# Expert value stage: earlier loads, gates laid out by 16 tokens, and gating four blocks at a time

## Chip, cores and metric

One core of a Trainium2 chip runs the whole kernel in one launch. The metric is the device time in microseconds, the median of repeated runs. A profiled execution of the same program gives the trace.

## The reference, cut to what matters

A decoder layer on 512 tokens of 1024 channels. First comes token mixing (differential attention and an mLSTM beside each other), then channel mixing by an expert retrieval, which is where the change lies:

```python
q = (ht @ w_q).reshape(T, PEER_HEADS, 2, PEER_DKEY // 2)
s = jnp.einsum('thpd,pnd->thpn', q, sub_keys).astype(jnp.float32)
sv, si = lax.top_k(s, PEER_TOPK)
...
eidx = i1 * N_KEYS + i2
g = jax.nn.softmax(cv, axis=-1)
...
act = jax.nn.gelu(jnp.einsum('cd,chkd->chk', hc, uc), approximate=False)   # uc = u_tab[ec]
...
return jnp.einsum('chk,chkd->cd', (gc * act).astype(hc.dtype), vc)         # vc = v_tab[ec]
```

Each token picks 8 x 16 of 16,384 experts. An expert is one row of u (layer 1) and one row of v (the value).

## The kernel before

**Dense and sparse tokens.** For 384 of the tokens (TD) the kernel computes all experts: 128 blocks of 128 experts, each block a product h2 x u, a gelu, a multiplication by the token's gate (zero for experts not chosen) and a product with v. For the other 128 tokens it gathers the chosen rows of u and v with indirect DMAs from POOL, one expert slot at a time, into a ring of four buffers (`gat`); VectorE forms the dot products (`gat<-gat,rows`) and later the sums of values (`accg`). `some(sp, n)` hands out these steps between the dense ones.

**Gates.** In the routing stage, before the value stage, `route` builds for each group of 16 tokens the gates of all experts with one-hot matmuls, four tokens to a PSUM tile. ScalarE evicts each tile to `gstage`, and a DMA writes the group to HBM (`gd`). There are 24 groups of four evictions.

**Layer 1.** The activations of blocks 0 to 71 are computed during routing and stored in HBM (`actd`). Those of blocks 72 to 127 are computed in the value stage.

**The value stage** runs rounds of four blocks, in the order q = 18 to 31 and then 0 to 17. `u_round` makes the activation tile `at` of a round (two buffers): for q of 18 and up by matmuls and a gelu on ScalarE, which is the first half of the stage; for q below 18 by two loads from `actd`, the second half. `v_round` multiplies one block of `at` at a time by its gates, splits the product into a high and a low half of 16 bits (`split`: ScalarE the high half, VectorE the low), loads and splits the 512 KB row block of v (`load_w`, three buffers `raw` shared with u, eight buffers for the split rows), and runs 18 matmuls into six PSUM accumulators (`out_part`). The gates of two rounds come in one load of 1.57 MB (`gblk`, two buffers left of the tag `big`). A gate of one block is every eighth element of that tile. The last round's blocks are kept for `last_part`, which closes the accumulators one by one and normalises the tokens.

All these loads leave from SP in one order. A scheduler sets the order of each engine's instructions when the kernel is built; TensorE's own order is that of the code. Each engine waits in order: what stands behind a waiting instruction waits too.

Of the kernel before, what the change touches and what calls it, by code (L numbers as in the profile page):

```python
# [8 lines left out]
F32 = mybir.dt.float32  # L9
# [62 lines left out]
FILL_H = 8400  # L72


class Ordered:
    """TensorE instructions, issued in the order in which they are written."""
# [26 lines left out]
def body(tc, x, c, w_ada, b_ada, wz, wif, b_if, conv_w, conv_b, lam, subg, mlg,  # L103
# [6 lines left out]
    with pool(name="cst", bufs=1) as cst, pool(name="wts", bufs=1) as wts, \  # L110
            pool(name="keep", bufs=1) as keep, pool(name="bg", bufs=1) as bg, \
            pool(name="wk", bufs=1) as wk, pool(name="dr", bufs=1, space=DRAM) as dr, \
            pool(name="ps", bufs=1, space=PSUM) as psp:

# [3 lines left out]
        def t4(name, shape=(128, 1024), dt=F32):  # L118
            return wk.tile(list(shape), dt, name=name, tag="t4", bufs=4)

        def t2(name, shape=(128, T), dt=F32):
            return wk.tile(list(shape), dt, name=name, tag="t2", bufs=6)
# [16 lines left out]
        # ---- constants  # L139
# [148 lines left out]
        # ---- adaLN modulation columns  # L288
# [44 lines left out]
        with pool(name="fr", bufs=1) as fr:  # L333
# [3 lines left out]
            # ---- LN1, its transposed, modulated, split copy, and the first projection  # L337
# [36 lines left out]
            # ---- small inputs  # L374
# [35 lines left out]
            # ---- projections of h1, as work between the steps of the branches  # L410
# [25 lines left out]
            # ---- differential attention, in steps of one head and one query block  # L436
# [84 lines left out]
            # ---- mLSTM  # L521
# [184 lines left out]
            # ---- merge  # L706
# [23 lines left out]
            # ---- order of the two branches  # L730
# [101 lines left out]
        # ---- PEER: routing and dense gates, beside the first expert activations  # L832
# [50 lines left out]
        with pool(name="rt", bufs=1) as rt:  # L883
# [50 lines left out]
            def route(t):  # L934
# [81 lines left out]
                for g in range(9):  # L1016
# [17 lines left out]
                    if pend is not None:  # L1034
                        pg, o1, ah, B = pend
                        half = stg[0][:, (pg % 2) * 2048:(pg % 2 + 1) * 2048]
                        st = half.rearrange("p (b t e) -> p b t e", b=16, t=16)
                        for q4 in range(4):
                            ps = ps_tr()
                            for k in range(4):  # L1040
# [3 lines left out]
                            A.activation(st[:, :, 4 * q4:4 * q4 + 4, :],  # L1044
                                         ps.rearrange("p t (b e) -> p b t e", b=16), AF.Copy,
# [8 lines left out]
            # ---- output projection, first residual and its two norms  # L1054
# [122 lines left out]
        # ---- PEER: expert outputs, beside the gathered experts of the first tokens  # L1177
# [4 lines left out]
        with pool(name="vp", bufs=1) as vp:  # L1182
            gat = big([128, 4, 1024], F32, "gat")
            accg = vp.tile([128, 1024], F32, name="accg")
            RV = 1.0 / (S_WT * S_V)
            order = list(range(N1 // 4, 32)) + list(range(N1 // 4))
            AT, GB = {}, {}
# [46 lines left out]
            def u_round(q_, rate=SP_U - SP_V):  # L1234
                at = vp.tile([128, 4, TD], F32, name="at", tag="at", bufs=2)
                AT[q_] = at
                if q_ < N1 // 4:
                    for k in range(2):
                        nc.sync.dma_start(at[:, 2 * k:2 * k + 2].rearrange("p a b -> p (a b)"),
                                          actd[2 * q_ + k])  # L1240
                else:
                    for i in range(4):
                        for _ in u_gen(4 * q_ + i, at[:, i]):
                            pass
# [122 lines left out]
```

## Time and profile before

| | |
|---|---|
| median of 3 runs | 1868.15 us (1867.54 to 1870.41) |
| span of the profiled execution | 1869.3 us |
| TensorE matmuls busy in it | 1718.7 us (92%) |
| VectorE busy | 1471.2 us (79%) |
| ScalarE busy | 822.8 us (44%) |
| GpSimd busy | 445.9 us (24%) |
| DMA, mean over the span | 259 GB/s |

The profiled execution is 1.15 us longer than the median of the runs. Shares over the span are means over stages with different limits; the stage of the change is cut out in the rows below.

### The profile page before, as it was taken

To read this page: it belongs to the slowest core of one execution; us is meant where nothing else is said; L and a number is where in the kernel's file an instruction comes from. 1 tells how busy PE (TensorE), PEld (TensorE's weight loads), DVE (VectorE), ACT (ScalarE), POOL (GpSimd) and SP (SyncE) were. 2 spreads that over 40 slices of the span, in tenths; PEclk is the share of its full clock that TensorE was granted. 3 is DMA by queue.
4 is the path that set the end of the run, shared out by engine and by line. 5 is a ranking of instruction groups with operands and counts; after the bars stand their busy time and mean duration, and the time that the engine had idled before them with its cause. 6 is when DMAs were issued, how large, how long until landed. Compare 5 with 4: busy or idle time off the path is not lost.

```text
span 1869.3 us, 26856 instructions
## 1 busy us (share of the span) xinstructions
PE 1718.7 (92%) x9937; PEld 920.4 (49%) x9937; DVE 1471.2 (79%) x2894; ACT 822.8 (44%) x1375; POOL 445.9 (24%) x296
## 2 busy tenths in 40 slices
PE   5999999989999899999989989999998998878895
PEld 2444455454444666666657544544554543333342
DVE  7778786786667798789899576977987777677689
ACT  4556766564343424547557432433332322222332
POOL 0000000010001000111101144544555634334443
PEclk9999999989999899999999999999999999989998
DMA  8555653447784457977959999899998888877874
GB/s 331 175 187 182 235 193 112 142 148 273 279 292 169 161 186 233 318 252 243 305 194 306 347 312 346 321 318 339 340 340 301 303 313 293 307 276 275 287 274 166
DMA packets 185477, 484.92 MB, mean 259 GB/s; under 512 B 15233, under 2 KB 64641, under 8 KB 185345
## 3 DMA queue, kind: packets, MB, share of 16 engines
q1 hardware_dynamic: 87280, 286.05, 44.5%
q0 software_dynamic: 36864, 134.23, 20.0%
q10 hardware_dynamic: 61200, 62.92, 9.8%
q8 instruction: 77, 1.26, 0.3%
q14 instruction: 56, 0.45, 0.1%
HBM read 418.14 MB, written 65.01 MB: 258 GB/s over the span
## 4 chain that ended last, share of the span: by engine, by line
PE 32%; DVE 25%; DMA 18%; issue 13%; POOL 7%; ACT 3%; ACTq 0%; DVEq 0%; POOLq 0%; SPq 0%
PE mm L97 21%; PE s L97 8%; DMA at<-actd 7%; DVE w L163 7%; POOL gat L859 7%; DVE accg L1227 4%; DMA gat<-in_v_dram,ev 4%; DMA gd<-gstage 2%; DVE at L1262 2%; PE tr L97 1%; DVE gat L867 1%; DMA raw<-in_v_dram 1%; PE tr L100 1%; DMA pre<-in_u_dram 1%; DMA gat<-in_urows_dram,eu 1%
## 5 line engine op out<-in xcount | busy, mean ns | idle before, releaser
L97 PEld LDWEIGHTS <-w 128*128 128x128 f16 x7176 | 694.1, 99 | 724.8 <-issue 120.4
L97 PE MATMUL mm<-h2T,w 128*128 128x384 f16 (+2 forms) x3288 | 564.0, 329 | 34.5 <-ACT at L851 22.5
L162 ACT ACTIVATE w<-raw 128x1024 f16<-128x1024 f32 x308 | 322.8, 1054 | 455.1 <-DMA raw<-in_v_dram 359.9
L163 DVE SCALAR_TENSOR_TENSOR w<-raw,w 128x1024 f16<-128x1024 f32 x308 | 375.2, 1220 | 100.2 <-ACT w L162 99.4
L97 PE MATMUL s<-w,w 128*128 128x512 f16 x1152 | 281.8, 389 | 48.5 <-DVE w L163 47.5
L859 POOL DMA_INDIRECT gat<-in_v_dram,ev x128 | 238.5, 1863 | 276.6 <-DVE accg L1227 265.8
L859 POOL DMA_INDIRECT gat<-in_urows_dram,eu x128 | 174.1, 1360 | 478.0 <-DVE gat L867 380.0
L97 PE MATMUL mm<-h1T,w 128*128 128x512 f16 x960 | 220.5, 381 | 1.8 <-DVE cva L618 1.8
L97 PE MATMUL tr<-w,w 128*128 128x512 f16 x768 | 186.2, 379 | 0.0
L1262 DVE TENSOR_TENSOR at<-at,gblk 128x384 f32<-128x384 f32 x128 | 108.6, 852 | 96.1 <-DMA at<-actd 90.0
L1227 DVE SCALAR_TENSOR_TENSOR accg<-gat,wg,accg 128x1024 f32<-128x1024 f32 x127 | 162.9, 1283 | 7.9 <-DMA gat<-in_v_dram,ev 7.8
L162 ACT ACTIVATE w<-at 128x384 f16<-128x384 f32 x128 | 65.7, 514 | 129.7 <-DVE at L1262 123.2
L867 DVE SCALAR_TENSOR_TENSOR gat<-gat,rows 128x1024 f32<-128x1024 f32 x89 | 108.1, 1219 | 12.5 <-DMA gat<-in_urows_dram,eu 12.4
L97 PE MATMUL mm<-w,h1T 128*128 128x512 f16 x456 | 107.7, 382 | 3.3 <-ACT h1T L162 1.8
L97 PE MATMUL o<-w,w 128*128 128x512 f16 x384 | 105.5, 386 | 0.0
L97 PEld LDWEIGHTS <-h1T 128*128 128x128 f16 x672 | 58.2, 98 | 66.0 <-issue 2.8
L159 POOL TENSOR_TENSOR ss<-ss,mhalf 128x4 f32<-128x4 f32 x8 | 8.1, 1017 | 314.4 <-DVE ss L504 283.4
L163 DVE SCALAR_TENSOR_TENSOR pre<-pre 128x1024 f16<-128x1024 f32 x44 | 53.8, 1223 | 34.8 <-ACT pre L162 33.7
L1044 ACT ACTIVATE gstage<-tr 128x512 f32<-128x512 f32 x96 | 56.6, 597 | 50.7 <-PE tr L97 39.6
L306 DVE SCALAR_TENSOR_TENSOR wad<-wad,silc 128x1024 f32<-128x1024 f32 x48 | 58.2, 1220 | 19.9 <-DMA wad<-in_w_ada_dram 19.9
L97 PEld LDWEIGHTS <-onehot 128*128 128x128 f16 x768 | 64.1, 148 | 19.1 <-issue 9.1
L97 PE MATMUL tr<-onehot 128*128 128x128 f16 x768 | 64.6, 227 | 9.0 <-ACT gstage L1044 7.6
(458 smaller groups left out, 1717.6 us busy)
## 6 DMA issues: line engine op xcount, KB each, us to landing
raw<-in_v_dram SPq DMA_DIRECT2D x128, 512.0 KB
raw<-in_u_dram SPq DMA_DIRECT2D x92, 512.0 KB
raw<-in_wz_dram SPq DMA_DIRECT2D x64, 512.0 KB
w<-us SPq DMA_DIRECT2D x52, 512.0 KB
wad<-in_w_ada_dram SPq DMA_DIRECT2D x48, 512.0 KB
gd<-gstage ACTq DMA_DIRECT2D x24, 1024.0 KB
us<-pre ACTq DMA_DIRECT2D x44, 512.0 KB
pre<-in_u_dram SPq DMA_DIRECT2D x36, 512.0 KB
```

Source lines behind the costliest of these rows:

```text
L97: self._link(self.tc.nc.tensor.matmul(*a, **k))
L100: self._link(self.tc.nc.tensor.transpose(*a, **k))
L159: G.tensor_tensor(o, i, mhalf[:, :i.shape[1]], op=ALU.pow)
L162: A.activation(hi, src, AF.Copy, scale=scale)
L163: V.scalar_tensor_tensor(lo, src, scale, hi, op0=ALU.mult, op1=ALU.subtract)
L306: V.scalar_tensor_tensor(w, w, 0.5, silc, op0=ALU.mult, op1=ALU.mult, accum_out=raw_[:, j:j + 1])
L859: P.before(G.indirect_dma_start(out=g_, out_offset=None, in_=table, in_offset=bass.IndirectOffsetOnAxis(ap=e[:, k:k + 1], axis=0)))
L867: V.scalar_tensor_tensor(g_, g_, 1.0, ring["h2r"], op0=ALU.mult, op1=ALU.mult, accum_out=wg[:, k:k + 1])
L1044: A.activation(st[:, :, 4 * q4:4 * q4 + 4, :], ps.rearrange("p t (b e) -> p b t e", b=16), AF.Copy, scale=1.0 / S_G)
L1227: V.scalar_tensor_tensor(accg, g_, wg[:, k:k + 1], accg, op0=ALU.mult, op1=ALU.add)
L1262: V.tensor_tensor(at[:, i], at[:, i], gt_[:, :, 4 * (q_ % 2) + i], op=ALU.mult)
```

## The change

- The scratch tiles of the first part (tags t4 and t2) get a pool of their own, which is closed before the value stage. The stage uses the room for a third buffer of `at` (AT_B = 3) and five buffers `vraw` for the rows of v (V_B = 5), apart from the three `raw` that remain for u.
- `gstage` and `gd` hold the gates by expert and then token: the 16 tokens of a group lie next to each other. The eviction therefore writes runs of four tokens and reads PSUM across four token tiles, one element from each in turn.
- The gates of two rounds are loaded in four parts, and the stored activations in two, from `ahead`, which is called between the value blocks two or three rounds before their use.
- `gate` multiplies all four blocks of a round at once (128 x 1536 instead of four times 128 x 384) and splits them at once into `w`, which has two buffers of a whole round instead of eight of one block. It is called for the next round after the second value block.

```diff
+AT_B = 3
+V_B = 5
...
+        front = ExitStack()
+        wt = front.enter_context(pool(name="wt", bufs=1))
...
-            return wk.tile(list(shape), dt, name=name, tag="t4", bufs=4)
+            return wt.tile(list(shape), dt, name=name, tag="t4", bufs=4)
...
-                        st = half.rearrange("p (b t e) -> p b t e", b=16, t=16)
+                        st = half.rearrange("p (i t) -> p i t", t=16)
...
-                            A.activation(st[:, :, 4 * q4:4 * q4 + 4, :],
-                                         ps.rearrange("p t (b e) -> p b t e", b=16), AF.Copy,
+                            A.activation(st[:, :, 4 * q4:4 * q4 + 4],
+                                         ps.rearrange("p t i -> p i t"), AF.Copy,
...
+        front.close()
...
-            def u_round(q_, rate=SP_U - SP_V):
-                at = vp.tile([128, 4, TD], F32, name="at", tag="at", bufs=2)
-                AT[q_] = at
-                if q_ < N1 // 4:
-                    for k in range(2):
-                        nc.sync.dma_start(at[:, 2 * k:2 * k + 2].rearrange("p a b -> p (a b)"),
-                                          actd[2 * q_ + k])
-                else:
-                    for i in range(4):
-                        for _ in u_gen(4 * q_ + i, at[:, i]):
-                            pass
-                        if q_ == order[0]:
-                            G.tensor_copy(gat[0:1, i, 0:1], at[0:1, i, 0:1])
-                        some(sp, rate)
+            def held(n):
+                return n < len(order) and order[n] < N1 // 4
+
+            def new_at(n):
+                AT[n] = vp.tile([128, 4, TD], F32, name="at", tag="at", bufs=AT_B)
+                return AT[n]
+
+            def act_load(n, k):
+                at = AT[n] if n in AT else new_at(n)
+                nc.sync.dma_start(at[:, 2 * k:2 * k + 2].rearrange("p a b -> p (a b)"),
+                                  actd[2 * order[n] + k])
+
+            def gate_load(n, k):
+                blk = order[n] // 2
+                if blk not in GB:
+                    GB[blk] = big([128, NG, 8, 16], F32, "gblk")
+                gs = slice(k * NG // 4, (k + 1) * NG // 4)
+                nc.sync.dma_start(GB[blk][:, gs].rearrange("p g e t -> p g (e t)"),
+                                  gd[gs, blk].rearrange("g p f -> p g f"))
+
+            def ahead(n, i):
+                if held(n + 2) and i % 2 == 0:
+                    act_load(n + 2, i // 2)
+                if n % 2 == 1 and i > 1 and n + 3 < len(order):
+                    gate_load(n + 3, i - 2)
+                if n % 2 == 0 and i % 2 == 0 and n + 2 < len(order):
+                    gate_load(n + 2, 2 + i // 2)
+
+            def u_round(n, rate=SP_U - SP_V):
+                at = new_at(n)
+                for i in range(4):
+                    for _ in u_gen(4 * order[n] + i, at[:, i]):
+                        pass
+                    if n == 0:
+                        G.tensor_copy(gat[0:1, i, 0:1], at[0:1, i, 0:1])
+                    some(sp, rate)
+
+            def gate(n):
+                q_, at = order[n], AT.pop(n)
+                av = at.rearrange("p a (g t) -> p a g t", t=16)
+                e = slice(4 * (q_ % 2), 4 * (q_ % 2) + 4)
+                V.tensor_tensor(av, av, GB[q_ // 2][:, :, e].rearrange("p g e t -> p e g t"),
+                                op=ALU.mult)
+                w = vp.tile([128, 2, 4, TD], F16, name="w", tag="w", bufs=2)
+                split(w[:, 0], w[:, 1], at, S_WT)
+                WT[n] = w
 
             ACC = [[ps_s(), ps_s()], [ps_s(), ps_o()],
                    [ps_tr().rearrange("p a b -> p (a b)") for _ in range(2)]]
-
-            def v_round(q_, first, keep_ops=None):
-                blk = q_ // 2
-                if blk not in GB:
-                    gt_ = big([128, TD, 8], F32, "gblk")
-                    nc.sync.dma_start(gt_.rearrange("p (g t) e -> p g (t e)", g=TD // 16),
-                                      gd[:, blk].rearrange("g p f -> p g f"))
-                    GB.clear()
-                    GB[blk] = gt_
-                gt_, at = GB[blk], AT[q_]
+            BANKS = [(t, b) for t in range(3) for b in range(2)]
+
+            def load_v(i2):
+                raw = vp.tile([128, 1024], F32, name="vraw", tag="vraw", bufs=V_B)
+                nc.sync.dma_start(raw, v[i2])
+                w = wts.tile([128, 2, 1024], F16, name="w2", tag="w2", bufs=8)
+                split(w[:, 0], w[:, 1], raw, S_V)
+                return w[:, 0], w[:, 1]
+
+            def out_part(op, tiles, start, stop):
+                w, i, vv = op
+                for t, b in tiles:
+                    ts = slice(t * 128, (t + 1) * 128)
+                    s = slice(b * 512, (b + 1) * 512)
+                    mm3_one(ACC[t][b], (w[:, 0, i, ts], w[:, 1, i, ts], vv[0][:, s], vv[1][:, s]),
+                            start, stop)
+
+            def v_round(n, keep_ops=None):
+                w = WT.pop(n)
                 for i in range(4):
-                    V.tensor_tensor(at[:, i], at[:, i], gt_[:, :, 4 * (q_ % 2) + i], op=ALU.mult)
-                    w = vp.tile([128, 2, TD], F16, name="w", tag="w", bufs=W_B)
-                    split(w[:, 0], w[:, 1], at[:, i], S_WT)
-                    op = (w, load_w(v[4 * q_ + i], S_V))
+                    ahead(n, i)
+                    op = (w, i, load_v(4 * order[n] + i))
                     if keep_ops is not None:
                         keep_ops.append(op)
                         continue
-                    out_part(op, BANKS, first and i == 0, False)
+                    out_part(op, BANKS, n == 0 and i == 0, False)
                     some(sp, SP_V)
+                    if i == 1 and n + 1 < len(order):
+                        gate(n + 1)
 
...
-                    o = t4("fo")
+                    o = vp.tile([128, 1024], F32, name="fo", tag="vraw", bufs=V_B)
...
-            u_round(order[0], SP_0)
-            for n, q_ in enumerate(order):
-                if n + 1 < len(order):
-                    u_round(order[n + 1])
+            for k in range(6):
+                gate_load(k // 4 * 2, k % 4)
+            u_round(0, SP_0)
+            gate(0)
+            for n in range(len(order)):
+                if n + 1 < len(order) and not held(n + 1):
+                    u_round(n + 1)
                 if n == 2:
                     P.before(nc.sync.dma_start(lg, ln2g.to_broadcast([128, 1024])))
                     P.before(nc.sync.dma_start(lb, ln2b.to_broadcast([128, 1024])))
-                v_round(q_, n == 0, ops if n == len(order) - 1 else None)
+                v_round(n, ops if n == len(order) - 1 else None)
```

SP's order in the second half of the stage, two rounds before the change. `raw<-in_v_dram` is a row block of v, `gblk<-gd` the gates, `at<-actd` the stored activations:

```order
240 L1256 DMA gblk<-gd 128x24x128
241 L167 DMA raw<-in_v_dram 128x1024 x2
242 L1239 DMA at<-actd 128x768 x2
243 L167 DMA raw<-in_v_dram 128x1024 x4
244 L1239 DMA at<-actd 128x768 x2
245 L167 DMA raw<-in_v_dram 128x1024 x2
```

The same place of the changed kernel, two rounds:

```order
256 L1251 DMA at<-actd 128x768 x2
257 L1295 DMA vraw<-in_v_dram 128x1024 x2
258 L1259 DMA gblk<-gd 128x6x128
259 L1295 DMA vraw<-in_v_dram 128x1024
260 L1259 DMA gblk<-gd 128x6x128 x2
261 L1295 DMA vraw<-in_v_dram 128x1024
262 L1259 DMA gblk<-gd 128x6x128
263 L1251 DMA at<-actd 128x768 x2
264 L1295 DMA vraw<-in_v_dram 128x1024 x4
```

The gate load of two rounds is now spread in quarters between the value rows, and no longer one block a few rows ahead of the activations.

VectorE's order in the second half before the change, most of a round. `at<-at,gblk` is the gating of one block, `w<-at,w` its low half, `w<-raw,w` that of the value rows (printed with the number of its buffer), `accg<-gat,wg,accg` the sum of a gathered row:

```order
2157 L1262 TENSOR_TENSOR at<-at,gblk 128x384
2158 L163 SCALAR_TENSOR_TENSOR w<-at,w 128x384
2159 L163 SCALAR_TENSOR_TENSOR w_15910<-raw,w_15910 128x1024
2160 L1227 SCALAR_TENSOR_TENSOR accg<-gat,wg,accg 128x1024
2161 L163 SCALAR_TENSOR_TENSOR w<-at,w 128x384
2162 L163 SCALAR_TENSOR_TENSOR w_15939<-raw,w_15939 128x1024
2163 L1227 SCALAR_TENSOR_TENSOR accg<-gat,wg,accg 128x1024
2164 L163 SCALAR_TENSOR_TENSOR w<-at,w 128x384
2165 L163 SCALAR_TENSOR_TENSOR w_15968<-raw,w_15968 128x1024
2166 L1227 SCALAR_TENSOR_TENSOR accg<-gat,wg,accg 128x1024
2167 L1262 TENSOR_TENSOR at<-at,gblk 128x384
```

The last split of a round (row 2164) frees its `at`; the next round's first gating (row 2167) follows two instructions later. After the change, one whole round:

```order
1982 L1283 TENSOR_TENSOR at<-at,gblk 128x1536
1983 L169 SCALAR_TENSOR_TENSOR w_15548<-vraw,w_15548 128x1024
1984 L1235 SCALAR_TENSOR_TENSOR accg<-gat,wg,accg 128x1024
1985 L169 SCALAR_TENSOR_TENSOR w_15579<-vraw,w_15579 128x1024
1986 L1235 SCALAR_TENSOR_TENSOR accg<-gat,wg,accg 128x1024
1987 L169 SCALAR_TENSOR_TENSOR w<-at,w 128x1536
1988 L169 SCALAR_TENSOR_TENSOR w_15604<-vraw,w_15604 128x1024
1989 L1235 SCALAR_TENSOR_TENSOR accg<-gat,wg,accg 128x1024
1990 L169 SCALAR_TENSOR_TENSOR w_15631<-vraw,w_15631 128x1024
1991 L1235 SCALAR_TENSOR_TENSOR accg<-gat,wg,accg 128x1024
1992 L1283 TENSOR_TENSOR at<-at,gblk 128x1536
```

A round has one gating and one split, with four instructions between each. The split of row 1987 belongs to the tile that was gated two gatings earlier; it frees the buffer into which the load for the gating of row 1992 goes.

## Rows read from the trace of the kernel before

**Rows 1.** The page's first line.

```profile
span 1869.3 us, 26856 instructions
```

**Rows 2.** Windows: stretch, its length, each engine's busy time (count), TensorE's clock, DMA.

```profile
core 0: us, PE busy (x) PEld busy (x) DVE busy (x) ACT busy (x) POOL busy (x), PEclk, DMA share, GB/s
1040.00:1466.00 426.00, 403.54 (x2152) 212.74 (x2150) 338.27 (x436) 151.37 (x215) 203.10 (x141) 0.98 0.93 328
1466.00:1838.00 372.00, 323.51 (x1445) 143.95 (x1444) 277.55 (x309) 112.39 (x155) 161.32 (x80) 0.95 0.81 289
...
1200.00:1420.00 220.00, 213.98 (x1141) 112.11 (x1140) 188.18 (x237) 80.65 (x113) 113.50 (x77) 0.99 0.94 337
```

**Rows 3.** Waits of TensorE, 1030 to 1870 us: total, times, longest.

```profile
PE s L97 <- DVE w L163: 47.5, 18, 7.2
PE mm L97 <- ACT at L851: 22.5, 6, 5.7
```

**Rows 4.** Waits of VectorE, 1030 to 1870 us.

```profile
DVE at L1262 <- DMA at<-actd: 90.0, 17, 9.4
...
DVE accg L1227 <- DMA gat<-in_v_dram,ev: 7.8, 9, 4.2
```

**Rows 5.** Timeline of SP's issues: start, length, line, transfer.

```profile
1547.04 0.80 SPq L1239 DMA_DIRECT2D at<-actd  x2
...
1660.66 0.68 SPq L1256 DMA_DIRECT2D gblk<-gd  x1
...
1666.67 0.80 SPq L1239 DMA_DIRECT2D at<-actd  x2
1667.81 19.81 SPq L167 DMA_DIRECT2D raw<-in_v_dram  x4
1688.95 0.80 SPq L1239 DMA_DIRECT2D at<-actd  x2
...
1788.27 0.81 SPq L1239 DMA_DIRECT2D at<-actd  x2
```

**Rows 6.** Timeline of VectorE, two rounds; in brackets the idle time before.

```profile
1676.92 0.85 DVE L1262 TENSOR_TENSOR at<-at,gblk 128x384 f32<-128x384 f32 x1 [7.95 <-DMA at<-actd]
...
1688.38 0.55 DVE L163 SCALAR_TENSOR_TENSOR w<-at,w 128x384 f16<-128x384 f32 x1
...
1694.10 0.86 DVE L1262 TENSOR_TENSOR at<-at,gblk 128x384 f32<-128x384 f32 x1 [2.84 <-DMA at<-actd]
```

**Rows 7.** Timeline of TensorE in the same rounds.

```profile
1680.19 3.57 PE L97 MATMUL s<-w,w 128*128 128x512 f16 x8 [6.14 <-DVE w L163]
...
1686.03 2.11 PE L97 MATMUL s<-w,w 128*128 128x512 f16 x9
...
1689.92 2.11 PE L97 MATMUL s<-w,w 128*128 128x512 f16 x9
```

**Rows 8.** Groups by line and form, VectorE, 1466 to 1838 us: busy us, mean ns.

```profile
L1227 DVE SCALAR_TENSOR_TENSOR accg<-gat,wg,accg 128x1024 f32<-128x1024 f32 x81 | 103.9, 1282 | 4.2 <-DMA gat<-in_v_dram,ev 4.2
L163 DVE SCALAR_TENSOR_TENSOR w<-raw,w 128x1024 f16<-128x1024 f32 x76 | 92.8, 1221 | 0.2 <-ACT w L162 0.2
L1262 DVE TENSOR_TENSOR at<-at,gblk 128x384 f32<-128x384 f32 x76 | 64.5, 853 | 90.0 <-DMA at<-actd 90.0
L163 DVE SCALAR_TENSOR_TENSOR w<-at,w 128x384 f16<-128x384 f32 x76 | 42.1, 555 | 0.0
```

**Rows 9.** Groups of VectorE, 600 to 1870 us: other two-operand sums.

```profile
L1194 DVE TENSOR_TENSOR fo<-fo,ax 128x512 f32<-128x512 f32 x6 | 3.9, 685 | 0.0
...
L954 DVE TENSOR_TENSOR cd<-sv 128x128 f32<-128x128 f32 x4 | 1.1, 274 | 0.0
```

**Rows 10.** Groups of ScalarE, 600 to 1870 us.

```profile
L162 ACT ACTIVATE w<-at 128x384 f16<-128x384 f32 x128 | 65.7, 514 | 129.7 <-DVE at L1262 123.2 <-DVE accg L1227 5.7 <-DVE gat L867 0.8
L1044 ACT ACTIVATE gstage<-tr 128x512 f32<-128x512 f32 x96 | 56.6, 597 | 50.7 <-PE tr L97 39.6 <-DMA gd<-gstage 9.0 <-issue 1.6
```

**Rows 11.** Windows: a stretch of gate groups in the routing stage.

```profile
981.92:1002.00 20.08, 20.08 (x185) 14.96 (x184) 20.05 (x22) 13.28 (x21) 2.86 (x2) 1.00 0.87 276
```

**Rows 12.** Timeline of TensorE: one round of layer-1 matmuls.

```profile
1125.94 15.76 PE L97 MATMUL mm<-h2T,w 128*128 128x384 f16 x96
```

More of the change, by code (lines that the diff above doesn't have):

```diff
@@ L1 @@
+from contextlib import ExitStack
 import numpy as np
@@ L118, in t4 @@
         def t4(name, shape=(128, 1024), dt=F32):
-            return wk.tile(list(shape), dt, name=name, tag="t4", bufs=4)
+            return wt.tile(list(shape), dt, name=name, tag="t4", bufs=4)
         def t2(name, shape=(128, T), dt=F32):
-            return wk.tile(list(shape), dt, name=name, tag="t2", bufs=6)
+            return wt.tile(list(shape), dt, name=name, tag="t2", bufs=6)
         def small(name, n, bufs=4, dt=F32):
@@ L1185, in body @@
             RV = 1.0 / (S_WT * S_V)
+            NG = TD // 16
             order = list(range(N1 // 4, 32)) + list(range(N1 // 4))
-            AT, GB = {}, {}
+            AT, WT, GB = {}, {}, {}
             def finish(t, o, halves):
@@ L1279, in last_part @@
                         some(sp, 1000)
-                    o = t4("fo")
+                    o = vp.tile([128, 1024], F32, name="fo", tag="vraw", bufs=V_B)
                     finish(t + 1, o, lambda b, s: V.scalar_tensor_tensor(
                         o[:, s], ACC[t][b], RV, g2r[:, s], op0=ALU.mult, op1=ALU.mult))
-            BANKS = [(t, b) for t in range(3) for b in range(2)]
-            def out_part(op, tiles, start, stop):
-                w, vv = op
-                for t, b in tiles:
-                    ts = slice(t * 128, (t + 1) * 128)
-                    s = slice(b * 512, (b + 1) * 512)
-                    mm3_one(ACC[t][b], (w[:, 0, ts], w[:, 1, ts], vv[0][:, s], vv[1][:, s]),
-                            start, stop)
-            ops = []
-            u_round(order[0], SP_0)
-            for n, q_ in enumerate(order):
-                if n + 1 < len(order):
-                    u_round(order[n + 1])
+            ops = []
+            for k in range(6):
[5 more added lines that the diff above has]
+                    u_round(n + 1)
                 if n == 2:
```

## The prediction

> **What bounds the kernel now.** I first cut the end of the run, the expert value stage, out of the windows view, because every edit but one lies in it. It runs from about 1040 us to the last gather at about 1838 us; the profiled span ends at 1869.3 us [rows 1]. It has two halves [rows 2]. Up to 1466 us each round computes four layer-1 blocks and then four value blocks: TensorE is busy 403.54 of 426 us and DMA moves 328 GB/s at a share of 0.93. After that the layer-1 activations come back from HBM instead: 372 us, TensorE busy 323.51, DMA only 289 GB/s at 0.81. Neither is full in this second half, and that is the thing to explain.
>
> The waits views say who is late. TensorE waits 47.5 us for VectorE's low half of w (all in the second half) and 22.5 us for ScalarE's eviction (all in the first) [rows 3]. VectorE waits 90.0 us for the stored activations, 17 times, and only 7.8 us for gathered rows [rows 4].
>
> One pair of rounds shows why. The activation tile has two buffers, so the next load can only leave when the last tile of the round is split. SP sends it at 1666.67, behind a 1.57 MB gate load sent at 1660.66 in the same queue [rows 5]; VectorE stands 7.95 us until 1676.92, works through the round, splits the last tile at 1688.38 [rows 6]; the next load leaves at 1688.95 [rows 5] and VectorE starts at 1694.10 [rows 6]. So a round is a load, then VectorE's work, one after the other: L + W, with L = 10.25 and 5.15 us (with and without a gate load in front), and W = 1688.95 - 1676.92 = 12.0 us. (10.25 + 5.15) / 2 + 12.0 = 19.7 us, close to the (1788.27 - 1547.04) / 12 = 20.1 us that a round takes from load to load [rows 5]. While VectorE stands, the value rows behind it keep their three buffers, and SP spreads the next four value loads over 19.81 us [rows 5]: one late load dries up the queue. TensorE then sits 6.14 us, and its next 8 matmuls take 3.57 us [rows 7].
>
> The limits, from rows. A value block is 18 matmuls in 1689.92 - 1686.03 = 3.89 us [rows 7], 0.216 us each; a layer-1 matmul takes 15.76 / 96 = 0.164 us [rows 12]. First half: 2152 matmuls [rows 2], of them 1287 layer-1 and the rest value, are 398 us. Second half: 1445, of them 59 layer-1, are 309 us. DMA: 426 x 328 = 139.7 MB and 372 x 289 = 107.5 MB. Where the old loop kept the queue fed, from 1200 to 1420 us, it carried 337 GB/s at 0.94 [rows 2]. At that rate the halves need 415 and 319 us: DMA is the tighter limit in both, TensorE close behind.
>
> **The change, part by part.**
>
> *Three activation tiles, five value row buffers apart from the three that stay for u, quarter gate loads.* Bytes stay the same, and so do the 512 B pieces of the gate load. The order shows what the third tile buys: the load still leaves only after a round's split, but between that split and the gating that needs the load VectorE now has two value splits and two gather sums, 2 x (1.22 + 1.28) = 5.0 us [rows 8], and the gating itself stands two rounds ahead of its split. A round by this loop is L + gating + those four again + split = L + 1.8 + 5.0 + 1.8 = L + 8.6 instead of L + 12.0. With the old mean L of 7.7 that is 16.3 us, under what DMA needs for a round: eight rows of 0.524 MB (four value rows, four gathers) and 0.786 MB each of activations and gates, 5.8 MB or 17.1 us at 337. So the loop stops being the bound and DMA becomes it, with L a little longer. I take 17.3 us. Such rounds run from about 1507 to 1838 us, 331 / 20.1 = 16.5 of them: 16.5 x (20.1 - 17.3) = 46 us. The first half at 337 GB/s: 415, a gain of 11; I take 9, as its waits lie on u rows too. Bounds for both together: nothing, if the rate stays where it is (247 MB in 798 us, 310 GB/s [rows 2]), and 798 - 398 - 309 = 91 us, if TensorE never waits.
>
> *Gating by four, and the gate layout.* The old gate operand is read every eighth element: 853 ns for 384 elements, against 555 ns for the split of the same tile [rows 8]. The new one is read in runs of 16. A row with such runs costs 274 ns for 128 elements; a row without gaps 685 ns for 512 [rows 9]: on one line, 1.07 ns an element, so no penalty, and 1536 elements come to 1.78 us in place of 4 x 0.853 = 3.41. The split goes from 4 x 0.555 = 2.22 to about 1.76 us (slope (1221 - 555) / 640 = 1.04 ns). VectorE saves 2.1 us a round; 0.5 if the penalty stays, and then the loop is L + 10.2, still 17.9. Its round is 15.6 us now (4 x (1.282 + 1.221 + 0.853 + 0.555)) and 13.5 after, under DMA's 17.1, which hides it: 0 beyond the loop's term. Without that cover it would be worth 32 x 2.1 = 67 us at most. ScalarE's split becomes one piece of 1.5 us (4 x 0.514 before [rows 10]); an eviction behind it may come 1 us late in 14 rounds of the first half. I take 0, bound 14, as ScalarE is busy 151 of 426 us [rows 2].
>
> *New waits.* One gating now needs two activation loads and four quarters at once; behind it on VectorE stand value splits and gather sums, and TensorE waits for the splits. The quarters leave about two rounds ahead: 0. The w tile has two buffers of a whole round: its split waits until TensorE has left the round two before, one round (15.6 us) before it is needed, and takes 1.5 + 1.8 us: it fits.
>
> *Start of the stage.* Six quarters instead of one whole block go ahead of the first value rows: 0.8 MB / 337 = 2.3 us, and the first value load also waits for the old gather ring. The first value matmul is some 31 us of layer-1 work away. I take 3, bounds 0 and 8.
>
> *Gate eviction.* This edit lies before the stage: ScalarE now reads PSUM with a jump of 512 B at every element. It costs 0.597 us now, 96 times [rows 10]; no row shows the new read. Nearest: VectorE's gapped read, 853 against 555, factor 1.54, so 0.92 us. Lower bound no change; no row closes it above, so I carry a factor of 4 (2.4 us) in the last rival. In the gate groups TensorE is full and ScalarE busy 13.28 of 20.08 us [rows 11]. A group of four evictions lasts about 6.85 us; at 0.92 us ScalarE goes from 4.5 to 5.8 of 6.85. It fits; for late evictions I take 2 us.
>
> **Sum.** 46 + 9 - 3 - 2 = 50 us. 1869.3 - 50 = 1819.3. The runs' median is 1.15 us under the profiled span, so 1818 us.
>
> **The rivals.**
>
> *TensorE becomes the bound.* For: DMA's 734 us (247 MB / 337) are only 4% above TensorE's 707, and the loop allows 16.3 us a round. Against: both would have to be nearly perfect. 91 less 5, less some 6 of small waits: 80, so 1788 us. Chance 0.17.
>
> *Half the gain.* The queue stays one queue. If more is in flight, L grows: at L = 10.25 in every round the loop gives 18.9 us, 16.5 x 1.25 = 21 us, and with 5 from the first half less 5 it is 1848 us, or 1847 by the median. For: up to five value rows and four quarters can now stand in front of an activation load. Chance 0.16.
>
> *It doesn't do what it says.* At L = 20.1 - 8.6 = 11.5 us the loop is as slow as before: 1868 us. Against: 10.25 is with a whole gate block in front. Chance 0.04.
>
> *Slower: the gate eviction becomes the bound.* It eats the whole gain if each of the 24 groups grows by (46 + 9 - 3) / 24 = 2.2 us, that is ScalarE at 9.05 us a group, an eviction of 0.6 + (9.05 - 4.5) / 4 = 1.7 us, about three times now. At 2.4 us a group is 4.5 + 4 x 1.8 = 11.7 us, 24 x 4.85 = 116 us more, less 52: about 1933 us. For: the jump at every element. Against: a factor of 3 where the nearest row has 1.54. Chance 0.07. [...]
>
> **How the numbers follow.** Forecast 0.56 (1800 to 1834), then 0.17, 0.16, 0.04 and 0.07. A range of 1786 to 1849 leaves out the slower and no-change cases and the outer tails of the first two rivals, some 0.18 in all. This kernel can tell 0.2% (3.7 us) from no change. Faster: 0.56 + 0.17 + 0.16 = 0.89; same 0.04; slower 0.07.
>
> **What would show it.** Right: VectorE's wait for activations well under 90 us; DMA above 325 GB/s in the second half; held rounds of 17 to 18 us; TensorE's waits in pieces of 1 to 2 us; a gating of about 1.8 us. Wrong: a gate eviction above 1.2 us, with TensorE waiting before the gate matmuls; or VectorE waiting as long as before, for the same loads or for gates or value rows, with the DMA share still near 0.81: then the order of the queue, and not its depth, was the limit.

## The result and the profile after

The median went from 1868.66 to 1811.32 us, a ratio of 0.9686 (95% interval 0.9664 to 0.9709). The profiled execution has a span of 1808.8 us, 60.5 less than that of [rows 1]; the medians differ by 57.3.

To see where the 60.5 us came from I cut both traces at the same three events, which bound the two halves of the value stage: TensorE's first value matmul, the end of its last layer-1 matmul, and VectorE's first instruction of the last part (`fo<-s,rows`). After the change the three rows are these (start, length, line, operation; the layer-1 group ends at 1433.56 + 15.76 = 1449.32):

```profile
1075.48 2.11 PE L101 MATMUL s<-w,w 128*128 128x512 f16 x9
...
1433.56 15.76 PE L101 MATMUL mm<-h2T,w 128*128 128x384 f16 x96
```

```profile
1782.01 0.69 DVE L1330 SCALAR_TENSOR_TENSOR fo<-s,rows 128x512 f32<-128x512 f32 x1 [8.56 <-PE s L101]
```

Before, the same events lie at 1071.71, 1475.49 and 1841.77 us. So the start of the stage comes 3.8 us later, the first half shrinks from 403.8 to 373.8 us (30.0), the second from 366.3 to 332.7 (33.6), and what follows by 0.7. The windows between these events, before:

```profile
1071.70:1475.50 403.80, 381.84 (x2019) 199.74 (x2017) 327.07 (x420) 139.65 (x197) 197.34 (x134) 0.97 0.93 328
1475.50:1841.80 366.30, 317.81 (x1404) 139.99 (x1403) 274.49 (x305) 109.28 (x151) 160.74 (x79) 0.95 0.81 287
```

And after:

```profile
1075.50:1449.30 373.80, 373.80 (x2018) 197.32 (x2017) 311.10 (x346) 137.59 (x162) 198.65 (x134) 1.00 0.97 353
1449.30:1782.00 332.70, 306.96 (x1382) 136.35 (x1380) 244.06 (x192) 103.70 (x93) 164.04 (x78) 0.97 0.87 310
```

The first half is now TensorE and nothing else: busy 373.80 of 373.80 us, at a granted clock of 1.00, while DMA carries 353 GB/s. Before, TensorE stood five times in it for an eviction, 22.0 us in all, as near 1100 us. ScalarE waits for a value row and splits it, and only then evicts the layer-1 result that TensorE stands for; ScalarE, then TensorE:

```profile
1099.43 1.06 ACT L162 ACTIVATE w<-raw 128x1024 f16<-128x1024 f32 x1 [10.42 <-DMA raw<-in_v_dram]
1100.39 0.47 ACT L851 ACTIVATE at<-mm 128x384 f32<-128x384 f32 x1
```

```profile
1100.92 9.32 PE L97 MATMUL mm<-h2T,w 128*128 128x384 f16 x46 [5.70 <-ACT at L851]
```

After the change the second half still has holes. Its waits (TensorE's, then VectorE's, from 970 to 1810 us) answer to [rows 3, 4]:

```profile
PE s L101 <- DVE w L169: 25.7, 7, 5.4
...
PE mm L101 <- ACT at L857: 0.2, 1, 0.2
```

```profile
DVE at L1283 <- DMA at<-actd: 70.7, 10, 11.3
```

TensorE's waits for evictions are gone. VectorE's wait for activations is still 70.7 us, now in every second round. SP's and VectorE's timelines over one such pair, as [rows 5, 6] of before:

```profile
1590.42 0.80 SPq L1251 DMA_DIRECT2D at<-actd  x2
1591.56 2.66 SPq L1295 DMA_DIRECT2D vraw<-in_v_dram  x2
1596.75 0.38 SPq L1259 DMA_DIRECT2D gblk<-gd  x1
1597.88 0.33 SPq L1295 DMA_DIRECT2D vraw<-in_v_dram  x1
1598.27 1.08 SPq L1259 DMA_DIRECT2D gblk<-gd  x2
1600.22 3.61 SPq L1295 DMA_DIRECT2D vraw<-in_v_dram  x1
1603.88 0.43 SPq L1259 DMA_DIRECT2D gblk<-gd  x1
1604.41 3.12 SPq L1251 DMA_DIRECT2D at<-actd  x2
1607.62 16.95 SPq L1295 DMA_DIRECT2D vraw<-in_v_dram  x4
1627.11 0.80 SPq L1251 DMA_DIRECT2D at<-actd  x2
```

```profile
1594.97 1.75 DVE L1283 TENSOR_TENSOR at<-at,gblk 128x1536 f32<-128x1536 f32 x1
...
1601.31 1.75 DVE L169 SCALAR_TENSOR_TENSOR w<-at,w 128x1536 f16<-128x1536 f32 x1
...
1618.99 1.76 DVE L1283 TENSOR_TENSOR at<-at,gblk 128x1536 f32<-128x1536 f32 x1 [11.27 <-DMA at<-actd]
```

The load that leaves at 1604.41, after the split at 1601.31, lands in front of the gating at 1618.99: L, the time from a load's issue to the gating that needs it, is 14.6 us: value rows and all four quarters of a gate block left in the 13 us ahead of it. The one before it has L = 4.55 (1590.42 to 1594.97) and held nobody up. A round takes (1627.11 - 1590.42) / 2 = 18.3 us. While VectorE stands for 11.27 us it splits no row and so frees no buffer, and right behind its wait DMA runs dry too: 60 and 4 GB/s in the two slices from 1618.8 us (40 slices of 2.05 us, from 1586 us):

```profile
DMA  7699999999999999107797899999999999316998
GB/s 250 206 369 353 264 364 384 373 391 362 328 387 397 363 399 390 60 4 252 224 391 296 284 397 293 296 332 377 363 384 386 382 405 408 160 10 250 286 352 323
```

The gating has the size that was foreseen, 1.755 us, and the eviction of the gates takes 0.598 us, as before ([rows 8, 10]):

```profile
L1283 DVE TENSOR_TENSOR at<-at,gblk 128x1536 f32<-128x1536 f32 x32 | 56.2, 1755 | 81.1 <-DMA at<-actd 70.7
...
L1050 ACT ACTIVATE gstage<-tr 128x512 f32<-128x512 f32 x96 | 56.5, 598 | 55.3 <-PE tr L101 37.9
```

The 3.8 us at the start have a wait of their own. Three of the six first gate quarters leave ahead of the last rows of u for the routing stage, and not only ahead of the first value rows. ScalarE then stands 5.42 us for a u row, until 1039.30 us, an eviction of the gates comes late behind it, and TensorE stands 4.28 us for that eviction; SP, then TensorE:

```profile
1024.86 4.69 SPq L1259 DMA_DIRECT2D gblk<-gd  x3
1029.65 3.14 SPq L173 DMA_DIRECT2D raw<-in_u_dram  x2
```

```profile
1040.90 1.12 PE L104 MATMUL tr<-ident,mcgt 128*128 128x128 f32 x4 [4.28 <-ACT gstage L1050]
```

From 1000 us to the first value matmul TensorE waits 9.4 us in all, 3.6 before; the execution was 2.2 us ahead when layer 1 began (629.39 against 631.55 us). That the quarters make this wait is read from the trace; no run sends them later.

### The profile page after: what moved, and what is told of

It reads as the page before. It is cut to its first block, busy times and chain, and to the rows that moved or that the text cites. A ratio compares the mean times of both kernels' runs of the same rounds, so it can differ in the third digit from the quotient of the medians.

```text
span 1808.8 us, 26501 instructions
## 1 busy us (share of the span) xinstructions
PE 1704.3 (94%) x9937; PEld 915.9 (51%) x9937; DVE 1423.5 (79%) x2702; ACT 813.1 (45%) x1279; POOL 452.6 (25%) x296
## 4 chain that ended last, share of the span: by engine, by line
PE 58%; DVE 16%; DMA 9%; issue 8%; POOL 4%; ACT 3%; ACTq 1%; SPq 0%; DVEq 0%; POOLq 0%
PE mm L101 32%; PE s L101 15%; PE tr L101 6%; POOL gat L865 3%; PE o L101 3%; DVE w L169 2%; DMA gat<-in_v_dram,ev 2%; DMA gd<-gstage 1%; PE tr L104 1%; DMA vraw<-in_v_dram 1%; DMA raw<-in_u_dram 1%; DVE accg L1235 1%; DVE gat L873 1%; ACTq L914 1%; DMA at<-actd 1%
## 5 line engine op out<-in xcount | busy, mean ns | idle before, releaser
L101 PE MATMUL mm<-h2T,w 128*128 128x384 f16 (+2 forms) x3288 | 558.0, 327 | 12.0 <-ACT ast L857 7.4
L101 PE MATMUL s<-w,w 128*128 128x512 f16 x1152 | 275.4, 384 | 25.7 <-DVE w L169 25.7
L865 POOL DMA_INDIRECT gat<-in_urows_dram,eu x128 | 179.5, 1403 | 447.6 <-DVE gat L873 352.0
L169 DVE SCALAR_TENSOR_TENSOR w<-raw,w 128x1024 f16<-128x1024 f32 x180 | 218.8, 1219 | 73.6 <-ACT w L168 73.1
L168 ACT ACTIVATE w<-vraw 128x1024 f16<-128x1024 f32 x128 | 134.9, 1055 | 284.2 <-DMA vraw<-in_v_dram 158.4
L168 ACT ACTIVATE w<-raw 128x1024 f16<-128x1024 f32 x180 | 188.2, 1053 | 85.6 <-DMA raw<-in_u_dram 34.1
L169 DVE SCALAR_TENSOR_TENSOR w<-vraw,w 128x1024 f16<-128x1024 f32 x128 | 155.2, 1217 | 20.2 <-ACT w L168 20.0
L1283 DVE TENSOR_TENSOR at<-at,gblk 128x1536 f32<-128x1536 f32 x32 | 56.2, 1755 | 81.1 <-DMA at<-actd 70.7
L873 DVE SCALAR_TENSOR_TENSOR gat<-gat,rows 128x1024 f32<-128x1024 f32 x89 | 107.9, 1220 | 12.5 <-DMA gat<-in_urows_dram,eu 12.4
L857 ACT ACTIVATE at<-mm 128x384 f32<-128x384 f32 x56 | 27.4, 489 | 129.8 <-PE mm L101 126.3
```

Of the source, the lines that this page charges most:

```text
L101: self._link(self.tc.nc.tensor.matmul(*a, **k))
L168: A.activation(hi, src, AF.Copy, scale=scale)
L169: V.scalar_tensor_tensor(lo, src, scale, hi, op0=ALU.mult, op1=ALU.subtract)
L857: A.activation(dst, ps[:, :TD], AF.Gelu, scale=RU)
L865: P.before(G.indirect_dma_start(out=g_, out_offset=None, in_=table, in_offset=bass.IndirectOffsetOnAxis(ap=e[:, k:k + 1], axis=0)))
L873: V.scalar_tensor_tensor(g_, g_, 1.0, ring["h2r"], op0=ALU.mult, op1=ALU.mult, accum_out=wg[:, k:k + 1])
```

## The experiments

Halves are cut at the three events above, in one profiled execution of each kernel. Ratios are to the kernel before, run beside each on the same chip (its medians lay between 1868.66 and 1870.92 us), with the 95% interval.

| kernel | median us | ratio | first half | second half |
|---|---|---|---|---|
| before | 1868.66 | 1 | 403.8 | 366.3 |
| the change | 1811.32 | 0.9686 (0.9664 to 0.9709) | 373.8 | 332.7 |
| at2 | 1808.10 | 0.9676 (0.9656 to 0.9696) | 373.8 | 331.6 |
| gate_whole | 1808.87 | 0.9664 (0.9645 to 0.9684) | 373.8 | 334.3 |
| raw_shared | 1833.38 | 0.9798 (0.9780 to 0.9816) | 394.6 | 330.0 |
| vb3 | 1828.08 | 0.9772 (0.9751 to 0.9794) | 396.8 | 331.5 |
| raw_whole | 1831.01 | 0.9778 (0.9730 to 0.9825) | 404.9 | 329.5 |
| old_layout | 1827.42 | 0.9770 (0.9722 to 0.9817) | 373.8 | 347.8 |
| before_quarters | 1857.35 | 0.9932 (0.9906 to 0.9958) | 397.6 | 368.0 |
| before_late | 2144.72 | 1.1446 (1.1387 to 1.1505) | 541.9 | 514.6 |
| before_lead | 1836.72 | 0.9814 (0.9790 to 0.9838) | 389.4 | 347.8 |
| late_plain | 1791.69 | 0.9574 (0.9551 to 0.9597) | 385.7 | 308.2 |
| late_at2 | 1776.51 | 0.9502 (0.9486 to 0.9517) | 373.8 | 297.9 |
| **gate_late** | **1773.79** | **0.9490 (0.9473 to 0.9507)** | 373.8 | 298.0 |

**gate_late: is it the loop or the transfer rate that still holds the second half?**

```diff
-                V.tensor_tensor(av, av, GB[q_ // 2][:, :, e].rearrange("p g e t -> p e g t"),
-                                op=ALU.mult)
+                P.before(V.tensor_tensor(av, av, GB[q_ // 2][:, :, e].rearrange("p g e t -> p e g t"),
+                                         op=ALU.mult))
```

`P.before` holds an instruction back until TensorE has reached its place in the code.

> The changed kernel, with the gating of a round held back on VectorE until TensorE has reached the place where the code calls it (in the middle of the round before its use); the split follows three instructions later instead of ten. Theory (the load loop still bounds the second half: a load waits for a split, the next gating stands four instructions behind that split): the load then has some 27 VectorE instructions to land, VectorE's 70.7 us of waits for activations and TensorE's 25.7 us for w go to under 10 us, the second half runs at TensorE's 15.6 us a round, and the time falls by 20 to 26 us, to 1785 to 1791. Rival (DMA is the limit, 5.8 MB a round at the 337 GB/s that I predicted with): 17.2 us a round, a fall of at most 15 us, to 1796 or more, with DMA's share at 0.95 in the second half.

It is the loop, and more hung on it than I had expected. VectorE's wait for activations is gone, and the second half is TensorE alone; windows of the two halves:

```profile
1072.20:1446.10 373.90, 373.90 (x2019) 197.35 (x2017) 314.48 (x350) 136.66 (x163) 212.59 (x135) 1.00 0.97 353
1446.10:1744.00 297.90, 297.90 (x1381) 134.96 (x1380) 243.24 (x189) 105.59 (x93) 124.62 (x76) 1.00 0.94 346
```

The fall is 37.5 us and not 20 to 26: besides TensorE's 25.7 us of waits, 306.96 - 297.90 = 9.1 us of its busy time went for the same matmuls, since its clock stays at 1.00 (0.97 in the changed kernel). The rest, some 3 us, lies outside the second half. The rival fell too: DMA carried 346 GB/s, and the rounds run at TensorE's pace. This kernel beats both.

**at2: what is the third activation tile worth?**

```diff
-AT_B = 3
+AT_B = 2
```

> The changed kernel with two activation tiles instead of three (the scheduler then gates one round ahead of the split instead of two; between the split that frees a tile and the gating that needs its load stand the same four instructions). Theory (the loop is L + gating + four + split whatever the number of tiles, so it was the gating and split of a whole round at once that shortened it): within 6 us of the changed kernel, 1808 to 1818, and the second half's rounds still 18 us. Rival (the third tile is what took the loop apart, as the prediction had it): the second half goes back toward 20 us a round, +25 to +35 us, 1836 to 1846.

Nothing that can be measured: 3 us less in the median, second halves within 1.1 us. The scheduler uses the third tile to place the gating a round earlier, and the same four instructions stay between the split that frees a tile and the gating that needs its load; VectorE waits as long:

```profile
DVE at L1283 <- DMA at<-actd: 72.9, 12, 12.1
```

**raw_shared, gate_whole, vb3, raw_whole: what freed the first half?**

```diff
 # raw_shared: the body of load_v
+                return load_w(v[i2], S_V)
 # gate_whole: in gate_load
-                gs = slice(k * NG // 4, (k + 1) * NG // 4)
+                if k > 0:
+                    return
+                gs = slice(0, NG)
 # vb3
-V_B = 5
+V_B = 3
 # raw_whole: raw_shared and gate_whole
```

> The changed kernel with the rows of v back in the ring of three buffers that they shared with the rows of u. Theory (in the first half TensorE lost time where a gate load of 1.57 MB stood before a value row and an eviction stood behind that row's split on ScalarE; the quarters cured it): under 8 us slower, TensorE's waits for the eviction of the activations stay under 5 us. Rival (the thin ring was the cause): the first half gives its 30 us back, 1836 to 1842, with 15 to 25 us of TensorE waiting for the eviction.

> The changed kernel with the gates of two rounds in one load of 1.57 MB, sent where the first quarter was sent. Theory (the burst was the cause in the first half): TensorE waits for the eviction of the activations again in every second round of the first half, six times 2 to 5 us, and the time is 10 to 30 us longer. Rival (five value rows in stock ride over a burst that takes 4.5 us at 350 GB/s; the thin ring was the cause): within 5 us of the changed kernel.

> The changed kernel with three value row buffers in place of five, still apart from the three for u. Theory (what counted in the first half is that rows of u and v no longer wait for each other in one ring): within 6 us of the changed kernel, the first half at 374 to 378 us. Rival (it is the depth): the first half at 385 us or more, +12 to +22 us.

> The changed kernel with both the shared ring of three row buffers and the whole gate load of 1.57 MB. Theory (each of the two alone covers part of the other: burst and thin ring together make the first half's loss): the first half goes to 400 to 408 us as in the kernel before, some 8 to 12 us more than with the shared ring alone, 1840 to 1850. Rival (only the ring matters): within 4 us of the run with the shared ring alone, 1830 to 1837.

My theories fell in all four medians: the burst, and in vb3 the ring that u and v share. With five value rows of their own a whole gate load costs nothing in the half (373.8). With three, shared or apart, the half is at 394.6 or 396.8 (so it gives 21 or 23 of the 30 us back, not all), and the eviction waits are back; TensorE's waits of raw_shared, then of vb3:

```profile
PE mm L101 <- ACT at L857: 14.9, 6, 6.8
```

```profile
PE mm L101 <- ACT at L857: 17.5, 6, 5.2
```

What counts is the depth of the ring. In the rows of before at 1099.43 us an eviction of layer 1 stands behind the split of a value row, for which ScalarE waited 10.42 us. ScalarE's waits for value rows from 1060 to 1480 us, before, after, and in vb3:

```profile
ACT w L162 <- DMA raw<-in_v_dram: 123.0, 29, 15.9
```

```profile
ACT w L168 <- DMA vraw<-in_v_dram: 11.9, 4, 8.9
```

```profile
ACT w L168 <- DMA vraw<-in_v_dram: 110.0, 17, 14.3
```

The burst adds to a thin ring, 404.9 against 394.6, as the theory of raw_whole had it for the half. Its median doesn't show this: its stage starts at 1073.91 us and that of raw_shared at 1080.71. What makes these 6.8 us stays open. Kernels with the same loads up to there start from 1071.68 (late_at2) to 1077.41 us (vb3), so starts differ by almost as much without whole loads.

**old_layout: what is the layout worth?** (The staging tile, the HBM array, the gate tile and the gating's operand go back to token, then expert.)

```diff
-                V.tensor_tensor(av, av, GB[q_ // 2][:, :, e].rearrange("p g e t -> p e g t"),
+                V.tensor_tensor(av, av, GB[q_ // 2][:, :, :, e].rearrange("p g t e -> p e g t"),
                                 op=ALU.mult)
```

> The changed kernel with the gates by token and then expert again, in the staging tile, in HBM and in the gating's operand; the order of VectorE's instructions is the same. Theory (the gating stands in the loop of the second half, and reads every eighth element): the gating takes 3.2 to 3.4 us in place of 1.76, and the second half grows by 1.5 us in each of 16 rounds, +20 to +26 us, 1831 to 1837. Rival (the gating's time is covered while VectorE waits for the load): within 5 us. The eviction of the gates stays at 0.60 us either way.

The theory, a little smaller: the gating takes 2.96 us, 1.20 more, and the second half grows by 15.1 us, 0.9 in each of some 16.5 rounds. The gating stands in the loop, and little covers it. Group of VectorE, 1450 to 1790 us:

```profile
L1283 DVE TENSOR_TENSOR at<-at,gblk 128x1536 f32<-128x1536 f32 x19 | 56.2, 2956 | 67.3 <-DMA at<-actd 67.3
```

**before_quarters: one part alone in the kernel before.**

```diff
                 for i in range(4):
+                    if q_ % 2 == 1 and q_ != order[-1]:
+                        gate_load((blk + 1) % 16, i)
```

> The kernel before with the gate load cut in quarters, one ahead of each value row of the round before. Theory (in the first half a value row of the thin shared ring comes late behind 1.57 MB, and the eviction behind its split on ScalarE with it): the first half goes from 403.8 to about 390 us, TensorE's 22.0 us of waits for the eviction there fall below 10; in the second half the loop keeps L + 12.0 with a mean L near 6 in place of 7.7, some 10 to 25 us; together 1830 to 1855. Rival (the ring of three is what matters, whatever stands in front of it): the first half stays above 400 us and the time above 1855.

Between the two, and a miss for the second half. The first half loses 6.2 us, the eviction waits only fall from 22.0 to 17.0; the second half doesn't gain (368.0), VectorE waits 90.9 us for activations as in [rows 4]. The other 9.4 us of the profiled span lie ahead of the stage's first value matmul; 6.2 of them are already there at the first wait of the gate groups (771.15 against 777.30 us), ahead of any gate load, so I don't credit them to the edit.

**before_late and before_lead: the order of VectorE alone in the kernel before.**

```diff
 # before_late
+                    P.before(V.tensor_tensor(at[:, i], at[:, i], gt_[:, :, 4 * (q_ % 2) + i], op=ALU.mult))
 # before_lead: after(r, mark) orders r behind a matmul kept in marks
+                    r = V.tensor_tensor(at[:, i], at[:, i], gt_[:, :, 4 * (q_ % 2) + i], op=ALU.mult)
+                    marks.append(P.prev)
+                    if len(marks) > 3:
+                        P.after(r, marks[-4])
```

> The kernel before with one thing changed: each gating is held back on VectorE until TensorE has reached its place in the code. No third tile, no new layout, no batching, no quarters. Theory (the second half was bound by the loop load, gating, split, load, and the order of VectorE alone takes it apart): a load now has some 17 VectorE instructions to land, VectorE's 90.0 us of waits for activations fall below 20 us, the second half loses 35 to 60 of its 366 us, the first half stays, 1808 to 1833. Rival (with two tiles, three row buffers and whole gate loads the queue stays as dry as before): less than 10 us faster, 1858 or more.

> The kernel before, each gating held back on VectorE until TensorE has come within three value blocks of its use (the run that held it back to the block itself left no lead, and TensorE waited in every block). Nothing else of the change. Theory (the order of VectorE alone makes the loop): a load has 18 VectorE instructions to land, no wait of VectorE for activations is left beyond 15 us in all, the second half goes from 366 to 310 to 330 us and the first half stays at 395 to 405: 1812 to 1838. Rival (the shared ring of three and the whole gate loads keep the queue dry): the second half stays above 350 us, 1853 or more.

The first was a mistake of mine that teaches something: `v_round` calls the gating right ahead of the block's own matmuls, so holding it there leaves no lead. The loop was gone (VectorE shows no wait for activations) and the time was 274 us longer, for TensorE now waits in nearly every block (120 and 119 times) for ScalarE's and then VectorE's half of w:

```profile
1706.83 0.61 PE L97 MATMUL s<-w,w 128*128 128x512 f16 x2 [1.61 <-ACT w L162]
1708.15 3.17 PE L97 MATMUL s<-w,w 128*128 128x512 f16 x7 [0.71 <-DVE w L163]
```

With a lead of three blocks the same edit is worth 32 us and no wait for activations is left. The second half falls by 18.5 us, to 347.8, between theory (310 to 330) and rival (above 350). The time fell into the theory's range only because the first half, which was to stay, lost 14.4 us too (its eviction waits go from 22.0 to 11.6). What stands in the second half now is a wait in every second round, as 5.54 and 5.14 us here, for ScalarE's half of w. ScalarE waits for a value row 16 times in this half, 94.0 us in all and 12.6 at most, and I take its half of w to stand behind the split of such a row, as VectorE's does (1761.21 us the row's split, behind a wait of 5.83, and 1762.35 that of w). It looks like the thin ring of the first half; this kernel was not tried with more row buffers. TensorE in two of these rounds:

```profile
1540.14 1.03 PE L104 MATMUL s<-w,w 128*128 128x512 f16 x2 [5.54 <-ACT w L169]
...
1578.33 1.03 PE L104 MATMUL s<-w,w 128*128 128x512 f16 x2 [5.14 <-ACT w L169]
```

**late_plain and late_at2: what does one need once the loop is gone?** late_plain is gate_late with AT_B = 2, whole gate loads and the old layout; late_at2 is gate_late with AT_B = 2 alone.

> The late gating of the fastest run with three parts of the change undone at once: two activation tiles, whole gate loads, gates by token and then expert. What is left of the change is the own ring of five value rows, the gating and split of a round at once, and the earlier place of the loads in the code. Theory (with the loop gone VectorE has time to spare, so a gating of 2.96 us, a burst of 1.57 MB and a missing third tile cost nothing): 1770 to 1780, TensorE waiting under 5 us in the stage. Rival (one of them still counts): 1785 or more, with VectorE or TensorE waiting for activations or gates.

> The late gating of the fastest run with two activation tiles instead of three, everything else of the change kept. Theory (even without the loop the third tile is spare: a load has two rounds less four instructions to land): within 5 us of the fastest run, 1769 to 1779, TensorE waiting under 3 us in the stage; then the 18 us that the run with three parts undone lost belong to the whole gate loads and the slower gating. Rival (the third tile counts once nothing else binds, above all where the first half gives way to the second): 1785 or more, with a wait of TensorE near 1480 us.

late_plain was a miss: 18 us slower than gate_late, with 13.3 us of TensorE waiting for evictions again and one wait of 6.03 us at 1482 us. late_at2 says that the third tile alone has no part in that: 1776.51 (1772.29 to 1777.93) against 1773.79 (1772.89 to 1776.88), halves equal to 0.1 us. So whole loads or the slower gating make the 18 us; which of the two, or whether it takes the two tiles beside them, was not tried. What its trace adds is that ScalarE waits 65.9 us for rows of u from 1075 to 1461 us, against 5.5 from 1060 to 1480 us in the changed kernel: u has kept its ring of three.

## Why the prediction was right, and where it was not

The median lay 6.7 us under the forecast and inside the likeliest case. The terms, against the profiled execution:

| term | predicted | measured |
|---|---|---|
| second half | -46 | -33.6 |
| first half | -9 | -30.0 |
| start and gate eviction | +5 | +3.8 |
| rest | 0 | -0.7 |
| sum | -50 | -60.5 |

**That the sum came so near is in part luck.** The second half gave 12.4 us less than its term and the first 21.0 us more. Of the five signs that were named for being right, only the gating's time came. VectorE's wait for activations is 70.7 us and not well under 90, DMA moves 310 GB/s in the second half and not over 325, a round takes 18.3 us and not 17 to 18, and TensorE's seven waits average 3.7 us and not 1 to 2.

**The loop was the right bound of the kernel before, but it did not give way to DMA.** It still bounds the second half: once gate_late takes it apart, the second half falls by another 34.7 us, while DMA carries 346 GB/s. Its formula fits, L + 8.6 with the two L of the pair: (4.55 + 14.58) / 2 + 8.6 = 18.2 us; measured 18.3. That fit is a weak test, as both L are read from the same rounds; gate_late is the strong one.

**L was mis-sized.** I took the old mean of 7.7 us, with which the loop drops under DMA's 17.3 us a round; L came out at 9.6. The rival with half the gain had this mechanism, more in the queue ahead of an activation load, at 10.25. (20.1 - 18.3) x 16.5 = 30 us of the measured 33.6.

**The third tile was given the credit wrongly.** What shortened the loop is that the gating is cheap, and, by what is left over, that a round is gated and split at once: old_layout takes 15.1 of the 33.6 us back, at2 and gate_whole none; no run undoes the batching alone. The four instructions that I counted between split and gating are there with two tiles as well, as the order of such a kernel would have told me.

**"DMA is the tighter limit in both" failed.** I read 337 GB/s, the best stretch of before, as the most that the queue can carry; the changed kernel carried 353 over 374 us. The old rate was what a stage paced by waits had asked for. Single slices of 2.05 us above reach more: many lie over 353, the highest at 408. With 353 the first half is TensorE's, which was the first rival, and it held in that half: 30 us in place of 9. The 22.5 us of [rows 3] were the sign; I let the transfer rate overrule them. They came from the thin ring, and the five rows removed them: with the five rows whole gate loads cost the half nothing (373.8 us in gate_whole), and the quarters alone took 6.2 us off it.

**The start had the right size by other waits.** TensorE waits 5.8 us longer ahead of the stage, 4.3 of them for the eviction behind a late u row, where I had put 3 us for the quarters ahead of the value rows and 2 for late evictions.

**The layout came as foreseen.** Gating 1.755 for 1.78 us, split 1.751 for 1.76, no penalty in runs of 16. For the case that the penalty stays I had left the gating at 4 x 0.853 = 3.41 us; batched and strided it takes 2.96, 0.45 less. But the layout was to be hidden under DMA beyond the loop's term; with the loop as the bound 0.9 of its 1.2 us show in every round. Per element, single words 32 B apart took 2956 / 1536 = 1.92 ns (old_layout), and runs of 16 took 1755 / 1536 = 1.14.

**The slower rival fell:** the eviction takes 0.598 us with its jump at every element and 0.597 before ([rows 10]), where I had put 0.92. The trace shows no cost of that jump in ScalarE's reads.

**A cost that I did not have:** TensorE's clock after a wait (0.50 behind the longest three, in the last section), 9.1 us of its busy time in the second half. In the changed kernel the loop sets the round all the same; the 9.1 us came back with the waits in gate_late.

## What to carry to other kernels

A buffer added to a load loop bought nothing here, where the scheduler spent it on placing the consumer earlier (1811.32 us with it, 1808.10 without): count the instructions between the one that frees a buffer and the one that needs its next load, on the engine that runs both, and hold the consumer back to where it is needed, with a lead that covers its own chain (half a round was right in the changed kernel; none cost 274 us in the one before). A rate that a stalled stage reached is no ceiling for the stage without the stall (337 GB/s before, 353 after). An engine that evicts PSUM and also splits loaded rows needs rows enough in stock: here the first half took 394.6 and 396.8 us with three and 373.8 with five, for a late row held up the eviction behind it.

## What the runs showed of the hardware

In the second half of the changed kernel the longer of TensorE's waits cost a second time, in its clock. Seven value matmuls took 3.17 us after each of the waits of 4.70, 5.09 and 5.38 us, at a granted clock of 0.50, and 1.69 us after one of 3.07, at 1.00:

```profile
1627.14 1.69 PE L101 MATMUL s<-w,w 128*128 128x512 f16 x7 [3.07 <-DVE w L169]
...
1663.77 3.17 PE L101 MATMUL s<-w,w 128*128 128x512 f16 x7 [5.38 <-DVE w L169]
```

DMA kept up 353 GB/s at a share of 0.97 in the first half after the change, beside a TensorE that was busy 373.80 of 373.80 us, with indirect gathers of 0.524 MB in the mix. And ScalarE read PSUM with a jump of 512 B at every element as fast as in runs of eight: 0.598 us an eviction after, 0.597 before.
